# FFN of an encoder trunk: the token operands of the fast matrix product are made between its first products, all first products stand ahead of the other five, and half of the normalising runs on ScalarE and GpSimd

## The chip, the cores and the metric

The kernel runs on one core of a Trainium2 chip. The engines of a core work in parallel, each through its own list of instructions in order: TensorE (PE) multiplies matrices, VectorE (DVE) and ScalarE (ACT) and GpSimd (POOL) work elementwise, and SyncE (SP) issues most DMAs. An instruction that waits holds up all that stands behind it on its engine. The metric is the device time of one execution in microseconds (us), the median of several runs. TensorE's granted clock is shown as a share of full speed; its two levels are 1.2 and 2.4 GHz, so 0.5 and 1.0.

## The reference

Two layers of a hybrid block on x (1 x 1024 tokens x 1024, float32). The part that the change touches is the feed-forward network (FFN):

```python
for i in range(DEPTH):                      # 2 layers
    ...                                     # attention, gating, convolution, w_out
    hf = rms_norm(x, norm_ffn_g[i]) @ w_gate_up[i]          # 1024 x 5632
    x = x + (jax.nn.silu(hf[..., :D_FF]) * hf[..., D_FF:]) @ w_down[i]   # D_FF = 2816
    ...                                     # gate and projection
```

Here `rms_norm(x, g)` is x times the reciprocal root of its mean square per token, times the gain g per column.

## The kernel before

Tiles lie with model columns on the 128 partitions and tokens along the free axis, so x is X[hf][m], m = 0 to 7 (blocks of 128 columns), hf = 0 or 1 (512 tokens each), every X tile 128 x 512. To keep float32 accuracy every operand is split into a high part (a rounded copy) and a low part (the rest), and a product takes three matmuls: high with high (L224), the token's low part with the weight's high part (L226), and the weight's low part with the token's high part (L228).

The product x @ w_gate_up is a seven-product scheme over 2 x 2 blocks: two halves of tokens, two halves of the inner dimension (HK = 4 blocks each), and two neighbouring column blocks. There are NP2 = 11 column pairs, each for the gate and for the up weights.

- **First products.** `first(j)` (L1110) makes two of the seven, for the first half of the tokens and the pair's first column block: two weights (gate, up) x two halves of the inner dimension x 12 matmuls = 48 matmuls, one PSUM bank for each group of 12. These use tokens without the norm's factor (tile hl), so the factor `bc` (one number per token, broadcast over partitions) is multiplied in by DVE while it evicts the bank: L1138 and L1140, then L1141 and L1145 combine. L1143 is the Silu on ACT. The sums go to DRAM (sum_d, act_d). The weights come through `load_w`: a DMA into raw, a high part wh, and a low part wl (L216), by default on ACT (L122) and DVE.
- **The other five.** They need combined token operands, which `token_forms(k)` (L1160) makes for k = 0 to 3: four normalisations of X tiles (L1157, in place: times gain, times bc), subtractions on DVE (L1167, L1169) and POOL (L1168, L1172), and five splits into high and low (tile tf; L122 on ACT and L125 on DVE). `rest(j)` (L1191) combines the raw weights (tile rw, loaded by `load_rest`, L1183) on POOL (L1228 to L1231), splits the results (L122, L125) and makes 5 x 12 matmuls for each of two weights, 120 in all.

The loop around them, per layer, begins in the attention's tail: w_out's second part is applied by `wo_second(0)`, then `first(0)` to `first(3)` (with the flag `ahead`, which has their wl made on POOL and wh on DVE), `first(4)` together with `wo_second(1)`, which ends with the norm of the second half: L292 sums on PE, L268 and L270 make the factor on DVE and POOL, L281 broadcasts it on PE and L298 copies it on ACT. Then come `token_forms(0)` to `token_forms(3)`, `first(5)` to `first(7)` (BEHIND = 3), and then `rest(j)` followed by `first(8 + j)` while there are any. The down product (w_down) follows.

The order of instructions on each engine is fixed when the program is built: a scheduler takes the program's order and the buffers that come free, and moves instructions past each other within that. Pools bound what runs ahead: raw, wh and wl have 3 buffers each, the PSUM pools ps_a and ps_t 3 and 4 banks (tiles pa and pt).

Of the kernel before, what the change touches and what calls it, by code (L numbers as in the profile page):

```python
# [43 lines left out]
PLE_LAG = 2  # L44
NP2 = NF // 2
AHEAD = 4
BEHIND = 3

C1 = 1
C2 = 2.0  # L50
# [21 lines left out]
def tile_encoder_trunk(ctx: ExitStack, tc: tile.TileContext, x, p, positions, norm_mix_g, w_in,  # L72
# [48 lines left out]
    def copy_h(dst, src, scale=1.0):  # L121
        nc.scalar.activation(dst, src, AF.Copy, scale=scale)  # L122
# [71 lines left out]
    def col(nme, layer, k):  # L194
        b, n = col_of[nme]
        c = b + layer * n + k
        return (cols0 if nme == "mix" else cols1)[:, c:c + 1]
# [264 lines left out]
    for layer in range(DEPTH):  # L462
# [656 lines left out]
        def first(j):  # L1119

            hl0, bc = nrm[0].hl, nrm[0].bc
            c0 = 2 * j * P
            ws = [load_w(rows_of(w_gate_up[layer], 0, NK, off + c0, P), (NK, P),
                         nc.gpsimd if ahead else None, nc.vector if ahead else None)
                  for off in (0, DFF)]
            a, sm = T("sg"), U("sm")
            for i, (wh, wl) in enumerate(ws):
                bank = BA if ahead else BU
                s1 = sm[:, HALF[i]]
                for h in range(2):  # L1130
                    b = bank()
                    for k in range(h * HK, (h + 1) * HK):
                        step_mm(b, (wh[:, k, :], wl[:, k, :]), hl0[k], k % HK == 0,
                                k % HK == HK - 1)
                        if k % 2 == 1:
                            bg.tick()
                    if h == 0:
                        nc.vector.tensor_tensor(out=s1, in0=b, in1=bc, op=ALU.mult)  # L1138
                    else:
                        nc.vector.tensor_tensor(out=b, in0=b, in1=bc, op=ALU.mult)  # L1140
                        nc.vector.tensor_tensor(out=b if i else a, in0=b, in1=s1, op=ALU.add)  # L1141
                if i == 0:
                    nc.scalar.activation(a, a, AF.Silu)  # L1143
            nc.scalar.dma_start(out=sum_d[j], in_=sm)
            nc.vector.tensor_tensor(out=a, in0=b, in1=a, op=ALU.mult)  # L1145
            nc.scalar.dma_start(out=act_d[2 * j][:, HALF[0]], in_=a)
# [9 lines left out]
        def normed(hf, m):  # L1156
            nc.vector.scalar_tensor_tensor(out=X[hf][m], in0=X[hf][m], scalar=col("ffn", layer, m),  # L1157
                                           in1=nrm[hf].bc, op0=ALU.mult, op1=ALU.mult)

        def token_forms(k):  # L1160

            for hf in range(2):
                for m in (k, k + HK):
                    normed(hf, m)
            b11, b21, b12, b22 = X[0][k], X[0][k + HK], X[1][k], X[1][k + HK]
            t1 = T("t1")
            nc.vector.tensor_tensor(out=t1, in0=b12, in1=b11, op=ALU.subtract)  # L1167
            nc.gpsimd.tensor_tensor(out=b12, in0=b22, in1=b12, op=ALU.subtract)  # L1168
            nc.vector.tensor_tensor(out=b11, in0=b22, in1=t1, op=ALU.subtract)  # L1169
            forms[0][k] = split(b11)  # L1170
            forms[1][k] = split(b12)
            nc.gpsimd.tensor_tensor(out=b21, in0=b21, in1=b11, op=ALU.subtract)  # L1172
            forms[2][k] = split(t1)
            forms[3][k] = split(b21)
            forms[4][k] = split(b22)
# [85 lines left out]
        first(AHEAD)  # L1261
        wo_second(1)
        ahead = False
        for k in range(HK):
            token_forms(k)
        for j in range(AHEAD + 1, AHEAD + 1 + BEHIND):
            first(j)
        for j in range(NP2):
            load_rest(j)
            rest(j)  # L1270
# [151 lines left out]
```

## Time and profile before

| | |
|---|---|
| median of 3 runs | 2505.62 us (2503.2 to 2507.15) |
| profiled execution, its own time | 2507.3 us |
| its span in the trace | 2505.5 us |
| PE / DVE / ACT / POOL busy | 93% / 60% / 37% / 29% |
| mean granted clock of PE | 0.967 |

The profile is of one execution. Layer 0's FFN runs roughly from 420 to 1090 us, layer 1's from 1655 us. A row of the waits says which engine and line stood idle for which other. In a timeline the number in brackets is the idle time ahead of the row's first instruction, and the arrow what ended it. Instructions that follow each other without a gap overlap at their ends, so the step from start to start, not the duration, counts in a run of them.

### The profile page before, as it was taken

The page shows a single profiled execution, that of the slowest core. Times are in us where ns is not written, and L with a number is a line of the kernel's source. Part 1 is how long each engine was busy: PE and PEld are TensorE (multiplying, and loading weights), DVE is VectorE, ACT ScalarE, POOL GpSimd, SP SyncE. Part 2 cuts the span into 40 slices and gives each one's busy share as a digit, 9 for nine tenths or more (in the row PEclk, how much of TensorE's full clock was granted, in tenths as well). Part 3 has the DMA queues.
Part 4 walks back from the last instruction along what each step waited for, and adds up shares of the span by engine and source line. Part 5 has one row for each costly group of instructions (what it writes and reads, how often), then busy time and mean ns, then how long its engine had stood idle before and what let it go on. Part 6 is the DMA issues. An engine that isn't in the chain of part 4 may idle for free. (4 is left out here: it accounts for less than half of the span.)

```text
span 2505.5 us, 30172 instructions
## 1 busy us (share of the span) xinstructions
PE 2327.1 (93%) x11404; PEld 1950.1 (78%) x11404; DVE 1493.4 (60%) x2307; ACT 915.8 (37%) x1610; POOL 730.1 (29%) x529
## 2 busy tenths in 40 slices
PE   7997977969999999999999898879689999999999
PEld 6996766847788888888789876768577888888887
DVE  7996676475665553626469666755856555526252
ACT  4346572132232243424323455612322222425242
POOL 4122415541344300104321233255424342001031
PEclk9998998989999999999999999989899999999999
DMA  6110513632543245543321123135345341736332
GB/s 200 44 55 9 177 34 97 214 110 93 190 163 110 94 161 174 176 135 106 100 68 39 35 76 110 58 119 181 101 160 173 118 146 52 234 123 210 100 91 70
DMA packets 237010, 294.78 MB, mean 118 GB/s; under 512 B 10644, under 2 KB 180208, under 8 KB 236864
## 3 DMA queue, kind: packets, MB, share of 16 engines
q1 hardware_dynamic: 217696, 248.55, 30.9%
q10 hardware_dynamic: 18688, 44.06, 4.8%
q8 instruction: 90, 1.47, 0.2%
q0 software_dynamic: 480, 0.24, 0.1%
q14 instruction: 56, 0.46, 0.1%
HBM read 228.84 MB, written 63.96 MB: 117 GB/s over the span
## 5 line engine op out<-in xcount | busy, mean ns | idle before, releaser
L216 DVE TENSOR_TENSOR wl<-raw,wh 128x1024 fp32r<-128x1024 f32 x172 | 216.7, 1260 | 255.3 <-ACT wh L122 249.8
L122 ACT ACTIVATE wh<-raw 128x1024 fp32r<-128x1024 f32 x172 | 182.0, 1058 | 438.2 <-PE pt L226 302.5
L226 PE MATMUL pt<-tf,wh 128*128 128x512 f32 x792 | 308.2, 389 | 0.0
L224 PE MATMUL pt<-tf,wh 128*128 128x512 f32 x792 | 306.1, 390 | 0.0
L228 PE MATMUL pt<-tf,wl 128*128 128x512 f32 x792 | 304.6, 389 | 0.0
L224 PE MATMUL pa<-tf,wh 128*128 128x512 f32 x704 | 277.3, 396 | 23.5 <-ACT wh L122 23.5
L264 POOL TENSOR_TENSOR st<-st,sq 128x512 f32<-128x512 f32 x82 | 121.4, 1482 | 596.9 <-ACT sq L263 594.9
L226 PE MATMUL pa<-tf,wh 128*128 128x512 f32 x704 | 278.2, 395 | 0.0
L228 PE MATMUL pa<-tf,wl 128*128 128x512 f32 x704 | 273.4, 393 | 0.0
L224 PE MATMUL pa<-hl,wh 128*128 128x512 f32 x564 | 228.1, 406 | 16.4 <-DVE sg L1141 10.9
L226 PE MATMUL pa<-hl,wh 128*128 128x512 f32 x564 | 225.6, 400 | 2.9 <-DVE hl L128 2.7
L228 PE MATMUL pa<-hl,wl 128*128 128x512 f32 x564 | 223.9, 397 | 0.0
L1228 POOL TENSOR_TENSOR ws<-rw,rw 128x512 f32<-128x512 f32 x44 | 70.1, 1593 | 410.6 <-DMA rw<-in_w_gate_up_dram 214.6
L608 PE MATMUL pa<-wh,hl 128*128 128x256 f32 x640 | 179.9, 287 | 7.0 <-ACT zq L621 3.7
L610 PE MATMUL pa<-wl,hl 128*128 128x256 f32 x640 | 181.9, 286 | 0.2 <-DVE wl L216 0.2
L611 PE MATMUL pa<-wh,hl 128*128 128x256 f32 x640 | 180.9, 286 | 0.0
L224 PEld LDWEIGHTS pa<-tf,wh 128*128 128x128 f32 x704 | 134.7, 191 | 55.1 <-ACT wh L122 26.9
L228 PEld LDWEIGHTS pt<-tf,wl 128*128 128x128 f32 x792 | 148.7, 188 | 31.1
L224 PEld LDWEIGHTS pt<-tf,wh 128*128 128x128 f32 x792 | 148.7, 188 | 30.9
L226 PEld LDWEIGHTS pt<-tf,wh 128*128 128x128 f32 x792 | 148.7, 188 | 30.6
L125 DVE TENSOR_TENSOR wl<-rw,wh 128x512 fp32r<-128x512 f32 x176 | 140.8, 804 | 32.5 <-ACT wh L122 32.4
L228 PEld LDWEIGHTS pa<-tf,wl 128*128 128x128 f32 x704 | 134.2, 191 | 28.6
(320 smaller groups left out, 5029.6 us busy)
## 6 DMA issues: line engine op xcount, KB each, us to landing
rw<-in_w_gate_up_dram SPq DMA_DIRECT2D x88, 512.0 KB, 6.9
raw<-in_w_down_dram SPq DMA_DIRECT2D x88, 512.0 KB, 3.6
raw<-in_w_gate_up_dram SPq DMA_DIRECT2D x44, 512.0 KB, 4.4
ac<-act SPq DMA_DIRECT2D x88, 256.0 KB, 4.3
raw<-in_w_ple_gate_dram SPq DMA_DIRECT2D x32, 512.0 KB, 4.2
raw<-in_w_in_dram SPq DMA_DIRECT2D x28, 512.0 KB, 3.8
raw<-in_w_out_dram SPq DMA_DIRECT2D x24, 512.0 KB, 4.2
sum<-sm ACTq DMA_DIRECT2D x22, 512.0 KB, 5.3
```

The lines of the kernel that those rows point to most:

```text
L122: nc.scalar.activation(dst, src, AF.Copy, scale=scale)
L125: nc.vector.tensor_tensor(out=dst, in0=src, in1=f(h), op=ALU.subtract)
L216: (eng or nc.vector).tensor_tensor(out=l, in0=raw, in1=f(h), op=ALU.subtract)
L224: nc.tensor.matmul(b, lhsT=wh, rhs=hl[:, 0:512], start=first, stop=False, skip_group_check=again)
L226: nc.tensor.matmul(b, lhsT=wh, rhs=hl[:, 512:1024], start=False, stop=False, skip_group_check=again)
L228: nc.tensor.matmul(b, lhsT=wl, rhs=hl[:, 0:512], start=False, stop=last, skip_group_check=again)
L264: (eng or nc.gpsimd).tensor_tensor(out=n.s, in0=n.s, in1=sq, op=ALU.add)
L608: nc.tensor.matmul(o, lhsT=x_[:, th], rhs=wh, start=(kc + k == 0), stop=False)
L610: nc.tensor.matmul(o, lhsT=x_[:, th], rhs=wl, start=False, stop=False)
L611: nc.tensor.matmul(o, lhsT=x_[:, tl], rhs=wh, start=False, stop=(kc == 1 and k == 3))
L1228: tt(out=s3, in0=a21, in1=a22, op=ALU.add)
```

## The change

BEHIND becomes 6, and the loop that comes after `wo_second(1)` makes all eleven first products before the first `rest`. `token_forms(k)` stands after `first(5 + k)` for k = 0 to 3. The first half's eight X tiles are no longer normalised by L1157 on DVE: ACT multiplies by the gain (a copy with a scale per partition, in place) and POOL by the factor (one multiply each, in place). And after the `ahead` part the gate weight's low part is made on POOL; the up weight's stays on DVE.

```diff
-BEHIND = 3
+BEHIND = 6
...
             ws = [load_w(rows_of(w_gate_up[layer], 0, NK, off + c0, P), (NK, P),
-                         nc.gpsimd if ahead else None, nc.vector if ahead else None)
+                         nc.gpsimd if ahead or off == 0 else None, nc.vector if ahead else None)
                   for off in (0, DFF)]
...
         def token_forms(k):
 
-            for hf in range(2):
-                for m in (k, k + HK):
-                    normed(hf, m)
+            for m in (k, k + HK):
+                normed(1, m)
...
         ahead = False
-        for k in range(HK):
-            token_forms(k)
-        for j in range(AHEAD + 1, AHEAD + 1 + BEHIND):
-            first(j)
+        for m in range(NK):
+            copy_h(X[0][m], X[0][m], col("ffn", layer, m))
+            nc.gpsimd.tensor_tensor(out=X[0][m], in0=X[0][m], in1=nrm[0].bc, op=ALU.mult)
+        for n in range(BEHIND):
+            first(AHEAD + 1 + n)
+            if n < HK:
+                token_forms(n)
         for j in range(NP2):
             load_rest(j)
             rest(j)
```

What stands in a row on POOL, in layer 0, where the norm of the first half ends (L270 makes its factor rcol_667; wl_687 and wl_696 are low parts of weights of `first(1)` and `first(2)`). Before:

```order
L264 TENSOR_TENSOR st_323_2500<-st_323_2500,sq_656_3982 128x512
L264 TENSOR_TENSOR st_323_2500<-st_323_2500,sq_662_4009 128x512
L264 TENSOR_TENSOR st_323_2500<-st_323_2500,sq_665_4029 128x512
L270 TENSOR_TENSOR rcol_667_4038<-ms_668_4039,mhalf_158 128x4
L216 TENSOR_TENSOR wl_687_4132<-raw_685_4130,wh_686_4131 128x1024
L216 TENSOR_TENSOR wl_696_4202<-raw_694_4200,wh_695_4201 128x1024
L216 TENSOR_TENSOR wl_699_4208<-raw_697_4206,wh_698_4207 128x1024
L216 TENSOR_TENSOR wl_708_4278<-raw_706_4276,wh_707_4277 128x1024
```

And with the change, where L1265 is the new multiply and st_323 holds the factor:

```order
L264 TENSOR_TENSOR st_323_2500<-st_323_2500,sq_656_3982 128x512
L264 TENSOR_TENSOR st_323_2500<-st_323_2500,sq_662_4009 128x512
L264 TENSOR_TENSOR st_323_2500<-st_323_2500,sq_665_4029 128x512
L270 TENSOR_TENSOR rcol_667_4038<-ms_668_4039,mhalf_158 128x4
L1265 TENSOR_TENSOR X_613_3776<-X_613_3776,st_323_2500 128x512 x2
L1265 TENSOR_TENSOR X_614_3777<-X_614_3777,st_323_2500 128x512 x2
L1265 TENSOR_TENSOR X_615_3778<-X_615_3778,st_323_2500 128x512 x2
L1265 TENSOR_TENSOR X_616_3779<-X_616_3779,st_323_2500 128x512 x2
L216 TENSOR_TENSOR wl_687_4132<-raw_685_4130,wh_686_4131 128x1024
L216 TENSOR_TENSOR wl_696_4202<-raw_694_4200,wh_695_4201 128x1024
L216 TENSOR_TENSOR wl_699_4208<-raw_697_4206,wh_698_4207 128x1024
```

The eight multiplies stand between the norm's factor and the low part wl_687; in the kernel before nothing stood there.

On DVE in layer 0, between the normalisation of the second half and the evictions of the first products that follow it (sm_796 before, and sm_772 with the change, hold the sums of `first(5)`; pa and pt are banks; tf tiles are parts of the token operands). Before, behind eight normalisations, eight subtractions and three low parts of weights:

```order
L1140 TENSOR_TENSOR pt_812_4843<-pt_812_4843,st_323_2500 128x512
L125 TENSOR_TENSOR tf_766_4621<-X_613_3776,tf_766_4621 128x512
L125 TENSOR_TENSOR tf_767_4624<-X_730_4428,tf_767_4624 128x512
L125 TENSOR_TENSOR tf_768_4628<-t1_765_4617,tf_768_4628 128x512
L125 TENSOR_TENSOR tf_769_4631<-X_615_3778,tf_769_4631 128x512
L125 TENSOR_TENSOR tf_770_4634<-X_732_4430,tf_770_4634 128x512
L125 TENSOR_TENSOR tf_772_4645<-X_613_3776,tf_772_4645 128x512
L125 TENSOR_TENSOR tf_773_4648<-X_730_4428,tf_773_4648 128x512
L125 TENSOR_TENSOR tf_774_4652<-t1_771_4641,tf_774_4652 128x512
L125 TENSOR_TENSOR tf_775_4655<-X_615_3778,tf_775_4655 128x512
L1138 TENSOR_TENSOR sm_796_4722<-pt_797_4723,st_323_2500 128x512
L1138 TENSOR_TENSOR sm_796_4722<-pt_799_4753,st_323_2500 128x512
```

With the change, directly behind the same eight normalisations:

```order
L1138 TENSOR_TENSOR sm_772_4642<-pt_773_4643,st_323_2500 128x512
L216 TENSOR_TENSOR wl_788_4735<-raw_786_4733,wh_787_4734 128x1024
L1141 TENSOR_TENSOR sg_771_4641<-pa_774_4657,sm_772_4642 128x512
L1166 TENSOR_TENSOR t1_777_4707<-X_730_4428,X_613_3776 128x512
L1138 TENSOR_TENSOR sm_772_4642<-pt_775_4673,st_323_2500 128x512
L1168 TENSOR_TENSOR X_613_3776<-X_732_4430,t1_777_4707 128x512
L1141 TENSOR_TENSOR pa_776_4687<-pa_776_4687,sm_772_4642 128x512
L216 TENSOR_TENSOR wl_806_4833<-raw_804_4831,wh_805_4832 128x1024
L1145 TENSOR_TENSOR sg_771_4641<-pa_776_4687,sg_771_4641 128x512
L125 TENSOR_TENSOR tf_778_4711<-X_613_3776,tf_778_4711 128x512
L125 TENSOR_TENSOR tf_779_4714<-X_730_4428,tf_779_4714 128x512
L1140 TENSOR_TENSOR pt_794_4785<-pt_794_4785,st_323_2500 128x512
```

An eviction (L1138, L1140, L1141, L1145) now stands after every one to three instructions on the operands; before, nine splits stood in a row ahead of the two L1138.

On SP, at the point where the raw weights of the first `rest` (rw and sm) are loaded; raw tiles are weights of first products or of the down product. Before:

```order
L211 DMA raw_855_5138<-in_w_gate_up_dram 128x8x128
L211 DMA raw_858_5144<-in_w_gate_up_dram 128x8x128
L211 DMA raw_897_5415<-in_w_gate_up_dram 128x8x128
L1184 DMA rw_827_4939<-in_w_gate_up_dram 128x4x256
L1184 DMA rw_828_4940<-in_w_gate_up_dram 128x4x256
L1187 DMA sm_825_4937<-sum0_119 128x1024
L1184 DMA rw_829_4944<-in_w_gate_up_dram 128x4x256
L1184 DMA rw_830_4945<-in_w_gate_up_dram 128x4x256
```

With the change:

```order
L211 DMA raw_837_5021<-in_w_gate_up_dram 128x8x128
L211 DMA raw_840_5027<-in_w_gate_up_dram 128x8x128
L211 DMA raw_849_5097<-in_w_gate_up_dram 128x8x128
L211 DMA raw_852_5103<-in_w_gate_up_dram 128x8x128
L211 DMA raw_1202_7422<-in_w_down_dram 128x1024
L211 DMA raw_1207_7433<-in_w_down_dram 128x1024
L211 DMA raw_1212_7444<-in_w_down_dram 128x1024
L1183 DMA rw_863_5175<-in_w_gate_up_dram 128x4x256
L1183 DMA rw_864_5176<-in_w_gate_up_dram 128x4x256
L1186 DMA sm_861_5173<-sum0_119 128x1024
L1183 DMA rw_865_5180<-in_w_gate_up_dram 128x4x256
L1183 DMA rw_866_5181<-in_w_gate_up_dram 128x4x256
```

The loads of the first `rest` have moved behind all loads of first products and behind three loads of w_down.

## Rows read from the trace of the kernel before

**Rows 1.** The page's first line, its busy times with their shares of the span.
```profile
span 2505.5 us, 30172 instructions
...
PE 2327.1 (93%) x11404; PEld 1950.1 (78%) x11404; DVE 1493.4 (60%) x2307; ACT 915.8 (37%) x1610; POOL 730.1 (29%) x529
```

**Rows 2.** The view of waits for PE over the whole span: engine, tile and line that stood idle, what it waited for, us in total, times, longest.
```profile
PE pt L224 <- DVE sm L1138: 36.9, 2, 18.6
PE pa L224 <- ACT wh L122: 23.5, 8, 4.2
...
PE pa L224 <- DVE sg L1141: 10.9, 3, 5.3
```

**Rows 3.** The table by stretches: start and end, length, then busy time (and number of instructions) of PE, PE's weight loads, DVE, ACT and POOL, the granted clock, DMA share and GB/s.
```profile
506.30:902.50 396.20, 366.67 (x1591) 300.47 (x1590) 244.21 (x342) 112.32 (x186) 143.18 (x96) 0.97 0.36 123
1741.50:2139.10 397.60, 366.37 (x1593) 300.97 (x1593) 248.88 (x343) 112.37 (x186) 142.95 (x96) 0.97 0.36 123
700.00:870.00 170.00, 170.00 (x752) 140.76 (x751) 92.50 (x144) 47.09 (x81) 71.35 (x52) 1.00 0.33 114
...
640.00:650.00 10.00, 8.82 (x32) 7.14 (x33) 9.16 (x9) 2.31 (x4) 8.61 (x6) 0.83 0.17 68
```

**Rows 4.** PE's timeline, the rows of layer 0's up-projection that begin after idle time: start, duration, engine, line, operation and tiles, and in brackets the idle time and its releaser.
```profile
535.88 0.76 PE L224 MATMUL pt<-hl,wh 128*128 128x512 f32 x1 [18.29 <-DVE sm L1138]
...
556.06 0.80 PE L224 MATMUL pa<-tf,wh 128*128 128x512 f32 x1 [3.94 <-ACT wh L122]
...
598.95 0.50 PE L224 MATMUL pa<-tf,wh 128*128 128x512 f32 x1 [2.97 <-ACT wh L122]
...
641.17 0.74 PE L224 MATMUL pa<-tf,wh 128*128 128x512 f32 x1 [2.21 <-ACT wh L122]
...
682.95 0.50 PE L224 MATMUL pa<-tf,wh 128*128 128x512 f32 x1 [1.80 <-ACT wh L122]
```

**Rows 5.** DVE's timeline in layer 0 from the broadcast of the second half's norm to the eviction that PE waits for.
```profile
507.22 5.39 DVE L1157 SCALAR_TENSOR_TENSOR X<-X,cols,st 128x512 f32<-128x512 f32 x8 [0.87 <-ACT st L298]
...
521.35 2.82 DVE L125 TENSOR_TENSOR tf<-X,tf 128x512 fp32r<-128x512 f32 x2
524.10 1.75 DVE L125 TENSOR_TENSOR tf<-t,tf 128x512 fp32r<-128x512 f32 x1
...
533.85 0.68 DVE L125 TENSOR_TENSOR tf<-t,tf 128x512 fp32r<-128x512 f32 x1
534.45 0.68 DVE L125 TENSOR_TENSOR tf<-X,tf 128x512 fp32r<-128x512 f32 x1
535.05 1.27 DVE L1138 TENSOR_TENSOR sm<-pt,st 128x512 f32<-128x512 f32 x2
```

**Rows 6.** POOL's timeline in layer 0: three elementwise operations, two low parts of weights, and the first subtractions of the token operands.
```profile
405.18 3.96 POOL L264 TENSOR_TENSOR st<-st,sq 128x512 f32<-128x512 f32 x3
...
422.76 2.78 POOL L216 TENSOR_TENSOR wl<-raw,wh 128x1024 fp32r<-128x1024 f32 x1 [8.15 <-DVE wh L215]
...
437.17 2.40 POOL L216 TENSOR_TENSOR wl<-raw,wh 128x1024 fp32r<-128x1024 f32 x1 [4.73 <-DVE wh L215]
...
513.29 13.67 POOL L1168 TENSOR_TENSOR X<-X,X 128x512 f32<-128x512 f32 x4 [7.44 <-DVE t L1167]
```

**Rows 7.** The table by stretches around the first half's normalisation, columns as in rows 3.
```profile
425.90:431.20 5.30, 0.01 (x1) 0.01 (x1) 5.30 (x10) 0.03 (x1) 1.12 (x1) 0.85 0.34 100
431.20:440.00 8.80, 8.80 (x28) 7.01 (x29) 4.39 (x7) 1.24 (x2) 3.65 (x2) 0.70 0.31 91
```

**Rows 8.** DVE's timeline around the first half's normalisation in layer 0, and the row of layer 1 that answers to the second.
```profile
420.62 1.41 DVE L1157 SCALAR_TENSOR_TENSOR X<-X,cols,st 128x512 f32<-128x512 f32 x2
...
422.54 3.55 DVE L1157 SCALAR_TENSOR_TENSOR X<-X,cols,st 128x512 f32<-128x512 f32 x2
...
426.62 2.72 DVE L1157 SCALAR_TENSOR_TENSOR X<-X,cols,st 128x512 f32<-128x512 f32 x4
...
437.68 0.69 DVE L1141 TENSOR_TENSOR sg<-pa,sm 128x512 f32<-128x512 f32 x1
...
1657.87 3.55 DVE L1157 SCALAR_TENSOR_TENSOR X<-X,cols,st 128x512 f32<-128x512 f32 x2
```

**Rows 9.** PE's timeline around the statistics of the second half's norm in layer 0.
```profile
503.61 0.94 PE L292 MATMUL po<-ones,st 128*128 128x1 f32 x8
...
505.91 0.65 PE L281 MATMUL pt<-ident,rcol 128*128 128x128 f32 x4 [0.30 <-POOL rcol L270]
```

**Rows 10.** POOL's timeline: the first combination of weights of the second `rest` in layer 0.
```profile
594.25 1.29 POOL L1228 TENSOR_TENSOR ws<-rw,rw 128x512 f32<-128x512 f32 x1 [38.61 <-DMA rw<-in_w_gate_up_dram]
```

**Rows 11.** The page's DMA issues: tiles, queue, number, KB each, median us from issue to landing.
```profile
rw<-in_w_gate_up_dram SPq DMA_DIRECT2D x88, 512.0 KB, 6.9
raw<-in_w_down_dram SPq DMA_DIRECT2D x88, 512.0 KB, 3.6
```

**Rows 12.** ACT's timeline: the copy of the first half's broadcast factor in layer 0.
```profile
418.79 0.59 ACT L298 COPY st<-pt 128x512 f32<-128x512 f32 x1 [6.04 <-PE pt L281]
```

**Rows 13.** The costliest groups of the page, POOL's combinations of weights: number, busy us, mean ns of one, idle before.
```profile
L1228 POOL TENSOR_TENSOR ws<-rw,rw 128x512 f32<-128x512 f32 x44 | 70.1, 1593 | 410.6 <-DMA rw<-in_w_gate_up_dram 214.6
```

## The prediction

> **What bounds the kernel now.** I read the page's shares first: TensorE (PE) is busy 93% of the span, VectorE (DVE) 60%, GpSimd (POOL) 29% [rows 1]. So time is won only where PE stands still or runs at its half clock, and I looked next for those places. The view of waits, taken for PE over the whole span, names three that belong to the FFN [rows 2]: a bank that DVE frees late by L1138 (36.9 us in two waits), weights that ScalarE (ACT) brings late by L122 (23.5 us in eight), and banks that wait for DVE's L1141 (10.9 us in three). The program runs the layer twice, so each is one place per layer or four.
>
> PE's stream shows the places in layer 0 [rows 4]: 18.29 us before 535.88, and then 3.94, 2.97, 2.21 and 1.80 us, each at the start of the five other products of a column pair (tile tf). The table by stretches gives what they cost [rows 3]. From 700 to 870 us PE has no idle time: 752 products in 170.00 us, 0.226 us each. The FFN's up-projection from 506.3 us (the end of the second half's norm broadcast) to 902.5 us (the first down product) holds 1591 of them: 1591 x 0.226 = 359.6 of 396.2 us, so 36.6 us are lost in layer 0; in layer 1 1593 x 0.226 = 360.0 of 397.6, so 37.6. The waits that are listed make only some 30 of each; the rest is the half clock behind them. Where 2.21 us of idle stand, the stretch of 640 to 650 us has 32 products in 8.82 us of busy time at a granted clock of 0.83: 32 x 0.226 = 7.2, so 1.6 us more are gone. I take 1.7 us for each gap of 2 to 4 us, and nothing for shorter ones.
>
> Why the 18 us: DVE's stream [rows 5] has eight normalisations (5.39 us), then subtractions and splits for all four sets of token operands, and the two evictions (L1138 at 535.05) for which PE waits stand behind them. They are also slow there: POOL's four subtractions of 513.29 take 13.67 us [rows 6] where three like operations at 405.18 took 3.96, and DVE's splits beside them 2.82 for two and 1.75 for one, where 533.85 to 535.05 shows a step of 0.60.
>
> A second place lies before it, in wo_second: the 5.30 us before 431.2 us, then 28 products in 8.80 us at clock 0.70 [rows 7]; 28 x 0.226 = 6.3, so 2.5 more, 7.8 us in all. There DVE normalises the first half (eight L1157, two of them 3.55 us instead of 1.41), with evictions queued behind [rows 8]. Layer 1 has the same 3.55 row.
>
> **The change, part by part.** *Normalising the first half leaves DVE.* Eight L1157 per layer, 1.41 + 3.55 + 2.72 us [rows 8], go. With them the 5.30 us of idle go, since the evictions are no longer behind them. ACT's eight scaled copies cost nothing: the order puts three of them ahead of the second half's norm work, and five fit in ACT's 6.04 us of idle before the broadcast's copy at 418.79 [rows 12]. POOL's eight multiplies begin when that copy is done, 419.4, and the order shows them ahead of the low part of the next weight (wl_687). At 1.30 each (3.96 / 3) they end at 429.8, the low part (2.40 uncontended) at 432.2 [rows 6]. PE, without its idle, has from 425.9 a whole bank (12 products) and six products that need only the high part: 18 x 0.226 = 4.1, so it waits from 430.0 to 432.2. With a little lengthening of POOL beside DVE's casts and of the clock I put 3.5 us against 7.8: a gain of 4.3 per layer. Bounds: no wait left (gain 7.8), and POOL held at the 3.42 us of 513.29 for all eight, 449.2 + 2.4 less 430.0 = 19 to 22 us (a loss of some 13).
>
> *Token operands between first products.* From the broadcast to the last first product PE now has 21 banks, 252 products, 57.0 us. I went down DVE's new order with the steps of before: 8 normalisations at 0.67, 28 subtractions and splits at 0.60, five low parts at 1.2, 32 evictions at 0.61: 5.4 + 16.8 + 6.0 + 19.5 = 47.7. Without contention DVE reaches each eviction 3 to 8 us before PE needs its bank. The tightest with POOL's work in front of it is the fourth column's first bank: DVE at 33.2, PE at 37.6, 4.4 of slack, and about 15 us of POOL's own work (four low parts, now POOL's for the gate, at 2.4, and four or five subtractions at 1.27) before it; at the last bank 48.2 against 56.6, slack 8.4, and 19.8 of POOL's work.
>
> What DVE loses beside POOL no row tells exactly. In 513.29 to 526.93 POOL had 5.2 us of own work and DVE lost 2.7 (2.82 + 1.75 for three steps of 0.60), half of it. Beside the low part at 422.76 (2.78 against 2.40) it lost 2.1, 3.55 against 1.41: nearly all of it [rows 6, 8]. Evictions from PSUM beside POOL's work were not slower: 0.69 at 437.68 [rows 8], inside POOL's 2.40 from 437.17 [rows 6]. I take one half, the row with the same operations: 7.6 less 4.4 = 3.2 us of PE's time. Ends: 0, and all of it.
>
> The Trainium skill, "SBUF — State Buffer", section "Who interferes with whom", says that a DVE instruction with two SBUF inputs and a GpSimd one that reads SBUF take turns at a shared port pair, the second blocked for the whole of the first. The 3.55 row agrees; at 513.29, where POOL lost 8.5 us itself, the cost is shared. By the rule alone DVE would lose up to all of POOL's time, the first rival below.
>
> *The norm's statistics.* Four products that stood between L292 and L281 while DVE and POOL worked out the factor [rows 9] stand elsewhere now: 4 x 0.226 = 0.9 us of idle.
>
> *Entry to the other five.* Before, each column pair's remaining products followed a first(8+j); the first four pairs began with a wait. Now all eleven stand together, as at 700 to 870 us, so I cost ten of the entries at nothing: the raw weights come while the pair before it runs. The first entry remains. The order puts three w_down loads ahead of the rw loads on SP's queue, and the third waits for the buffer of the last up weight, whose low part DVE makes at 44.6 without and about 53.5 with contention. An rw load lands 6.9 us later (median) [rows 11], 60.4; from POOL's first combination to PE's first product 4.7 us pass (594.25 to 598.95) [rows 4, 10]: 65.1. PE is through at 57.0 + 0.9 + 3.2 = 61.1. So 4.0 us of stall, and 1.7 of half clock. If the three w_down loads of 3.6 us delay rw one after the other, up to 8 us more; with a quick landing next to nothing.
>
> **Sum.** Left over per layer: 0.9 + 3.2 + 4.0 + 1.7 = 9.8 us. Layer 0: 36.6 - 9.8 + 4.3 = 31.1; layer 1: 37.6 - 9.8 + 4.3 = 32.1; together 63.2. The profiled execution took 2507.3 us over its span of 2505.5; its span becomes 2442.3 and its time 2444.1. Its time is 1.7 above the median of the runs, 2505.62, so I forecast 2505.6 - 63.2 = 2442.
>
> **Rivals.**
> (a) DVE is blocked for all of POOL's time. The loss before the last bank is 19.8 - 8.4 = 11.4 instead of 3.2, in two gaps of over 2 us (3.4 us of half clock), and the early wait grows by some 2.4: 14.0 per layer, 2442 + 28 = 2470. For it: the 3.55 row; against: the shared cost at 513.29. 20%.
> (b) The rw loads come late behind w_down: 8 us per layer, 2458. For it: SP's order; against: they are only delayed if DVE or the queue is. 17%.
> (c) Everything is hidden: per layer only 0.9 and 1 to 2 us of entry and early wait remain, about 2422. For it: DVE's slack at each bank. 8%.
> (d) Slower: GpSimd becomes the bound. Its multiplies stand ahead of a weight that PE waits for, and its gate low parts feed the first products. At 2.63 times their lone price (3.42 / 1.30) with DVE blocked throughout, the early place loses about 13 and the later one still gains about 13: no change, 2505. Above that factor the kernel is slower: at 3.5, POOL's 19.8 us become 69 for PE's 57, another 12 per layer, and the early place loses some 9 more than at 2.63: 21 per layer less is 2547. For it: 13.67 us for four; against: at the early place DVE then has mostly evictions and casts, and POOL's combinations of weights, of the same shape and beside DVE's splits, take 1.59 in the mean of 44 [rows 13]. 4%.
> (e) The change does not do what it says: the order has the operands between the first products and no first product behind a remaining one, so it does; what can still be is a scheduler's shift in layer 1's attention, a few us either way. 1%.
>
> **How the numbers follow.** The forecast has 50%. Eight times in ten: from 2424, a little above (c), to 2476, past (a); (d) and the tails are left out. What a measurement of this kernel can tell is about 0.2%, 5 us; (a), (b), (c) and the forecast all lie far below that line: faster 0.95, same 0.02, slower 0.03.
>
> **What will show it.** Right: the wait on L1138 of 18 us is gone in both layers, the ones on L122 shrink from eight to two; POOL's eight multiplies take 10 to 13 us; the stretch from broadcast to down product is 370 us or less, of it the remaining products about 11 x 27.1 = 298 without a gap; one wait at their start. Wrong: multiplies of 2 us and more with PE waiting for the low part behind them, waits of PE for evictions adding up to over 8 us per layer among the first products, an entry wait over 8 us, or new gaps between the pairs.

## The result and the profile after

The changed kernel takes 2445.27 us in the median of four runs (2441.96 to 2445.79), the kernel before 2506.39 beside it (2503.2 to 2508.02): a ratio of 0.9755 with a 95% interval of 0.9738 to 0.9772, so 61 us less. The forecast was 2442 us. The profiled execution took 2445.79 us with a span of 2444.0.

The page's first lines and the view of waits for PE over the whole span, which answer to [rows 1, 2]:

```profile
span 2444.0 us, 30173 instructions
...
PE 2314.7 (95%) x11404; PEld 1942.1 (79%) x11404; DVE 1452.7 (59%) x2279; ACT 925.5 (38%) x1626; POOL 757.3 (31%) x557
```

```profile
PE pa L224 <- ACT wh L122: 11.1, 2, 6.2
...
PE pa L224 <- DVE sg L1141: 4.7, 3, 1.6
...
PE pa L228 <- POOL wl L216: 2.7, 2, 1.4
...
PE pt L228 <- DVE wl L216: 2.4, 1, 2.4
...
PE pa L224 <- DVE sm L1138: 1.9, 4, 1.1
```

The 36.9 us behind L1138 have become 1.9 us, in four short waits instead of two of 18 us. The 23.5 us behind L122 have become 11.1, one wait per layer, at the entry to the other five products. The waits on POOL's and DVE's low parts (L216) are new. In layer 0 the rows of PE that answer to [rows 4, 7, 9]:

```profile
431.54 0.50 PE L224 MATMUL pa<-hl,wh 128*128 128x512 f32 x1 [1.57 <-DVE sg L1141]
433.64 0.80 PE L228 MATMUL pa<-hl,wl 128*128 128x512 f32 x1 [1.37 <-POOL wl L216]
...
504.15 0.65 PE L281 MATMUL pt<-ident,rcol 128*128 128x128 f32 x4 [1.35 <-POOL rcol L270]
527.58 0.50 PE L224 MATMUL pa<-hl,wh 128*128 128x512 f32 x1 [0.31 <-DVE sm L1138]
...
540.78 0.50 PE L224 MATMUL pa<-hl,wh 128*128 128x512 f32 x1 [1.09 <-DVE sm L1138]
...
556.05 0.50 PE L224 MATMUL pa<-hl,wh 128*128 128x512 f32 x1 [0.90 <-DVE sg L1145]
...
573.47 0.79 PE L224 MATMUL pa<-tf,wh 128*128 128x512 f32 x1 [6.22 <-ACT wh L122]
```

The table by stretches, columns as in [rows 3]: the two up-projections, then in layer 0 all first products behind the broadcast, their first ten microseconds, the early place, and the other five products with the ten microseconds at their start.

```profile
504.80:876.18 371.38, 362.86 (x1589) 298.20 (x1588) 233.96 (x337) 112.22 (x186) 142.91 (x100) 0.99 0.38 131
1706.23:2077.50 371.27, 362.35 (x1589) 298.46 (x1588) 234.35 (x338) 112.40 (x186) 141.29 (x100) 0.99 0.39 131
...
504.80:567.24 62.44, 60.14 (x252) 47.73 (x251) 61.36 (x77) 24.33 (x36) 21.29 (x12) 0.97 0.45 146
504.80:515.00 10.20, 10.20 (x39) 8.28 (x39) 9.55 (x12) 3.91 (x5) 2.14 (x1) 0.83 0.11 34
420.61:440.00 19.39, 16.45 (x64) 12.86 (x65) 9.75 (x14) 2.55 (x3) 17.66 (x11) 0.91 0.31 99
573.47:875.00 301.53, 301.53 (x1331) 249.62 (x1332) 170.05 (x258) 85.91 (x147) 117.19 (x85) 0.99 0.35 122
573.47:583.47 10.00, 10.00 (x37) 8.15 (x38) 8.14 (x10) 1.62 (x3) 7.70 (x6) 0.84 0.91 308
```

The up-projection has gone from 396.2 and 397.6 us to 371.4 and 371.3. From 573.47 on PE has no idle time: the entries to the later pairs cost nothing. In the first products DVE is busy 61.36 of 62.44 us, so it has next to nothing to spare there, though PE waits for it only 2.3 us.

How the gain is spread over the program is best seen from fixed points of PE's stream, each taken from the start of a row of PE's timeline: *a* the attention's last broadcast before the FFN (L281 from the tile ar), *b* the broadcast of the second half's norm (L281 at 505.91 in [rows 9]), *c* the first down product, *d* the first statistics broadcast behind the down products; the last column goes to the start of PE's last row. Lengths in us for layer 0 and, from a of layer 1 on, layer 1:

| kernel | start to a | a to b (early place) | b to c (up-projection) | c to d | d to a of layer 1 | a to b | b to c | c to PE's last row |
|---|---|---|---|---|---|---|---|---|
| before | 405.2 | 100.7 | 396.6 | 250.1 | 487.6 | 101.0 | 397.7 | 361.4 |
| changed | 405.9 | 98.3 | 372.0 | 250.2 | 480.8 | 98.5 | 371.9 | 361.5 |
| order_only | 403.4 | 100.7 | 365.8 | 250.1 | 483.5 | 99.3 | 366.1 | 361.4 |
| norm_only | 406.3 | 97.5 | 399.2 | 250.1 | 482.1 | 97.5 | 400.1 | 361.4 |
| gate_dve | 402.9 | 97.4 | 366.1 | 250.2 | 484.2 | 97.6 | 366.2 | 361.4 |
| rw_early | 403.5 | 98.1 | 369.9 | 250.1 | 481.4 | 98.6 | 370.0 | 361.4 |
| pool_dummy | 402.5 | 97.0 | 379.3 | 250.2 | 481.0 | 97.7 | 376.5 | 361.5 |
| gate_rw | 405.0 | 97.4 | 369.4 | 250.1 | 481.4 | 97.2 | 366.0 | 361.5 |
| gate_wl1 | 407.7 | 91.7 | 365.8 | 250.1 | 481.6 | 92.6 | 367.0 | 361.4 |
| all_three | 404.4 | 92.4 | 370.2 | 250.1 | 488.6 | 92.5 | 366.3 | 361.4 |
| before_again | 403.2 | 100.4 | 393.9 | 250.2 | 484.4 | 100.4 | 398.8 | 361.4 |
| after_again | 403.6 | 98.1 | 373.7 | 250.1 | 482.5 | 98.4 | 372.0 | 361.4 |

The rows below the second are the experiments that follow; the last two are the two kernels once more, unchanged, and show how far a length varies by itself: up to 2.7 us in the up-projection (396.6 and 393.9 for the kernel before). Of the 61.5 us by which the spans differ, the up-projection gives 24.6 and 25.8, the early place 2.4 and 2.5, and 6.8 come from the stretch between d and layer 1's attention, in which nothing was changed; the start took 0.7 us longer.

### The profile page after: what moved, and what is told of

Same layout as the page of the kernel before. It is cut to its first block, busy times and chain, and to the rows that moved or that the text cites. A ratio compares the mean times of both kernels' runs of the same rounds, so it can differ in the third digit from the quotient of the medians.

```text
span 2444.0 us, 30173 instructions
## 1 busy us (share of the span) xinstructions
PE 2314.7 (95%) x11404; PEld 1942.1 (79%) x11404; DVE 1452.7 (59%) x2279; ACT 925.5 (38%) x1626; POOL 757.3 (31%) x557
## 5 line engine op out<-in xcount | busy, mean ns | idle before, releaser
L216 DVE TENSOR_TENSOR wl<-raw,wh 128x1024 fp32r<-128x1024 f32 x160 | 203.0, 1269 | 260.8 <-ACT wh L122 254.2
L122 ACT ACTIVATE wh<-raw 128x1024 fp32r<-128x1024 f32 x172 | 181.8, 1057 | 392.8 <-PE pt L226 260.9
L224 PE MATMUL pa<-tf,wh 128*128 128x512 f32 x704 | 274.0, 392 | 11.1 <-ACT wh L122 11.1
L226 PE MATMUL pa<-tf,wh 128*128 128x512 f32 x704 | 275.4, 391 | 0.0
L226 PEld LDWEIGHTS pt<-tf,wh 128*128 128x128 f32 x792 | 148.7, 188 | 30.8
L216 POOL TENSOR_TENSOR wl<-raw,wh 128x1024 fp32r<-128x1024 f32 x56 | 138.2, 2473 | 69.3 <-ACT wh L122 46.0
L122 ACT ACTIVATE wh<-rw 128x512 fp32r<-128x512 f32 x176 | 105.6, 622 | 141.3 <-PE pt L226 73.9
```

What stands on the lines that cost most here:

```text
L216: (eng or nc.vector).tensor_tensor(out=l, in0=raw, in1=f(h), op=ALU.subtract)
L224: nc.tensor.matmul(b, lhsT=wh, rhs=hl[:, 0:512], start=first, stop=False, skip_group_check=again)
L226: nc.tensor.matmul(b, lhsT=wh, rhs=hl[:, 512:1024], start=False, stop=False, skip_group_check=again)
```

## The experiments

**The order alone** (order_only), against the changed kernel:

```diff
-                         nc.gpsimd if ahead or off == 0 else None, ...
+                         nc.gpsimd if ahead else None, ...
...
-            for m in (k, k + HK):
-                normed(1, m)
+            for hf in range(2):
+                for m in (k, k + HK):
+                    normed(hf, m)
...
-        for m in range(NK):
-            copy_h(X[0][m], X[0][m], col("ffn", layer, m))
-            nc.gpsimd.tensor_tensor(out=X[0][m], in0=X[0][m], in1=nrm[0].bc, op=ALU.mult)
```

> Only the new order: all first products ahead with the token operands between them; both halves are normalised by L1157 on DVE and the gate's low parts stay on DVE. Theory: the order alone removes the 18 us in front of the late eviction and the three entries to the other five; the early place stays as before (5.3 us of idle and some 2.5 us of half clock per layer instead of the 1.6 + 1.4 us of idle and 2 to 3 us of half clock of the changed kernel), so 3 to 4 us per layer are given up: 2451 to 2453 us. Rival 1: without the relief of DVE by eight normalisations and four low parts the evictions are late again, with waits of PE of more than 5 us per layer among the first products: 2460 us or more. Rival 2: the normalising is worth nothing: 2445 us.

2438.5 us (2436.85 to 2440.87), ratio to before 0.9729 (0.9714 to 0.9743): less than the changed kernel (2441.96 to 2445.79), against all three expectations. The early place kept its 5.30 us of idle, as expected, and its 100.7 us (99.3 in layer 1). But the up-projection takes 365.8 us, 6.2 less than in the changed kernel. So the order alone gains 30.8 us there in layer 0, where the changed kernel gains 24.6: something else in the change gives some 6 us per layer back.

**The normalising alone** (norm_only): the ACT copies and POOL multiplies in the kernel before, with its old order.

```diff
+        for m in range(NK):
+            copy_h(X[0][m], X[0][m], col("ffn", layer, m))
+            nc.gpsimd.tensor_tensor(out=X[0][m], in0=X[0][m], in1=nrm[0].bc, op=ALU.mult)
         for k in range(HK):
             token_forms(k)
...
-            for hf in range(2):
-                for m in (k, k + HK):
-                    normed(hf, m)
+            for m in (k, k + HK):
+                normed(1, m)
```

> Only the moved normalising, in the old order: ACT's scaled copies and POOL's eight multiplies in place of the first half's L1157. Theory: the wait of 5.3 us in the early place shrinks to some 3 us in two parts, the waits of 18 us and the four entry waits per layer stay: 3 to 4 us per layer less than before, 2499 us (2496 to 2503). Rival: POOL's multiplies only move the wait from the eviction to the low part of the weight: 2506 us, no change.

2498.39 us (2495.29 to 2502.63), ratio 0.9971 (0.9958 to 0.9984), the time that the theory gave. The early place is shorter by 3.2 and 3.5 us as expected. The up-projection is longer by 2.6 and 2.4 us, which was not expected; as it varies by up to 2.7 us between the two traces of the kernel before, whether the edit has a part in it stays open. In this trace 5.5 us come from the stretch d to a, on which more below, so that the time came out as the theory gave it may in part be luck.

**The gate's low parts back on DVE** (gate_dve): the changed kernel without one of its edits.

```diff
-                         nc.gpsimd if ahead or off == 0 else None, nc.vector if ahead else None)
+                         nc.gpsimd if ahead else None, nc.vector if ahead else None)
```

> The changed kernel with the gate's low parts of the later first products on DVE again. Theory of exclusive turns (a POOL operation on SBUF holds up a DVE operation with two SBUF inputs until it ends): each low part on POOL costs DVE about 2 us of its 2.4 when it falls on such an operation, and 1.2 us when DVE makes it itself, so moving them gains nothing: 2445 us, within 4 us, and in the trace the eight subtractions on POOL delay DVE but no row of DVE's of 2.7 us or more is left. Rival: POOL's work runs mostly beside DVE's evictions from PSUM and is nearly free, so giving DVE six more low parts of 1.2 us per layer makes its evictions late: 4 to 6 us per layer more waiting of PE, 2453 to 2457 us.

2435.93 us (2432.53 to 2438.42), ratio 0.9717 (0.9702 to 0.9731), and its interval lies below that of the changed kernel. Neither expectation had this sign of that size: the edit that takes work from DVE costs 5.9 us of the up-projection in layer 0 and 5.7 in layer 1. The first products behind the broadcast in layer 0, the table by stretches of this run, of order_only and (above) of the changed kernel:

```profile
500.97:559.75 58.78, 57.71 (x252) 46.80 (x251) 57.93 (x81) 23.62 (x35) 13.55 (x10) 1.00 0.53 173
```

```profile
504.78:562.46 57.68, 57.67 (x252) 46.81 (x251) 56.85 (x81) 23.62 (x35) 14.56 (x10) 1.00 0.53 175
```

252 products take 58.78 and 57.68 us instead of 62.44; DVE makes four more low parts (81 instructions for 77) and is busy 3.4 and 4.5 us less. Most of the reason stands in the changed kernel's own rows. DVE's timeline:

```profile
513.10 2.71 DVE L1166 TENSOR_TENSOR t<-X,X 128x512 f32<-128x512 f32 x1
515.74 0.68 DVE L1138 TENSOR_TENSOR sm<-pt,st 128x512 f32<-128x512 f32 x1
516.34 1.39 DVE L1168 TENSOR_TENSOR X<-X,t 128x512 f32<-128x512 f32 x1
...
523.71 3.21 DVE L125 TENSOR_TENSOR tf<-X,tf 128x512 fp32r<-128x512 f32 x2
...
546.25 1.22 DVE L216 TENSOR_TENSOR wl<-raw,wh 128x1024 fp32r<-128x1024 f32 x1
```

and POOL's beside it:

```profile
512.86 2.40 POOL L216 TENSOR_TENSOR wl<-raw,wh 128x1024 fp32r<-128x1024 f32 x1 [8.76 <-ACT wh L122]
515.89 1.28 POOL L1167 TENSOR_TENSOR X<-X,X 128x512 f32<-128x512 f32 x1 [0.63 <-DVE t L1166]
...
523.37 2.40 POOL L216 TENSOR_TENSOR wl<-raw,wh 128x1024 fp32r<-128x1024 f32 x1 [4.27 <-ACT wh L122]
...
546.71 3.02 POOL L216 TENSOR_TENSOR wl<-raw,wh 128x1024 fp32r<-128x1024 f32 x1 [3.40 <-ACT wh L122]
```

POOL's low part ends at 512.86 + 2.40 = 515.26, and the subtraction that DVE began at 513.10 ends at 515.81, 0.55 later: it stood still for all of POOL's instruction and then ran its usual 0.6. The next one, L1168, ends at 517.73, 0.56 after POOL's end of 517.17; the first of the two splits at 523.71 waits for POOL's 525.77. The eviction from PSUM at 515.74, of which POOL's 515.89 covers all but the start, took its usual 0.68. POOL keeps its lone price of 2.40 and 1.28 where it began first; where DVE did, as with the low part of 546.25, POOL is the one that waits (3.02 us from 546.71). Adding up by how much DVE's rows in this stretch exceed their usual lengths (0.68 us for one operation of 128x512, 0.60 more for each that follows in the row, 1.22 for a low part; the eight L1157 take 5.39 us here, in gate_dve and in the kernel before, POOL standing idle beside them, and are left out) gives 11.4 us for POOL's 21.3, and in gate_dve, where no operation of 2.7 us is left among the first products, 3.8 us for 13.6.

Not all of the 5.9 us is this. The edit also changed PE's order at the broadcast. In gate_dve, as in order_only and in the kernel before [rows 9], four products stand between the statistics' matmuls (L292) and L281; in the changed kernel none do. L281 waits 1.35 us there, and in gate_dve:

```profile
500.32 0.65 PE L281 MATMUL pt<-ident,rcol 128*128 128x128 f32 x4 [0.30 <-POOL rcol L270]
```

The wait itself belongs to a to b. The half clock behind it, 39 products at 0.83 in the table above, costs 1.4 us of the 5.9. Of the rest, 2.2 us are the entry to the other five (4.00 us of idle instead of 6.22) and 1.2 the waits among the first products (1.07 instead of 2.30); some 1 us was not traced further.

Against order_only, which differs only in the place of the first half's normalising, gate_dve is 2.6 us faster. The runs of the two overlap, but a to b is 3.3 and 1.7 us shorter.

**POOL work that nobody waits for** (pool_dummy): gate_dve, with two operations added on POOL after each of the six first products. They write to a tile whose values are not used again, so the output stays the same.

```diff
+            if not ahead:
+                s = nrm[1].s
+                for i in range(2):
+                    nc.gpsimd.tensor_tensor(out=s, in0=s, in1=sm[:, HALF[i]], op=ALU.subtract)
             nc.scalar.dma_start(out=sum_d[j], in_=sm)
```

> The gate's low parts on DVE, as in the run gate_dve (2436 us), and two more operations of 128x512 on POOL after each of the six later first products, which subtract that product's sums from a tile that nobody reads any more; no other engine waits for them. They are 12 x 1.27 = 15.2 us of POOL's time per layer, about what the six low parts were (6 x 2.4). Theory: POOL's operations cost by holding up DVE's operations with two inputs in SBUF; what DVE loses between the broadcast and the first of the other five rises from 5 to about 10 to 13 us per layer, and the time from the broadcast to the first down product from 366 to 369 to 372 us: 2442 to 2447 us. Rival: the low parts cost because PE and SP wait for them, made later and slower on POOL; operations that nobody waits for cost nothing: 2436 us, 366 us.

2453.77 us (2452.07 to 2455.73), ratio 0.9798 (0.9783 to 0.9813). That is 18 us over gate_dve for operations whose results no engine reads, so the rival, by which such operations cost nothing, falls. L281 waits 0.30 us here as in gate_dve, so PE's order at the broadcast has no part in it. It is more than expected: the up-projection takes 379.3 and 376.5 us instead of 366. The row that shows it, the first products in layer 0:

```profile
500.17:568.20 68.03, 61.47 (x252) 49.21 (x251) 65.51 (x81) 24.46 (x36) 29.13 (x19) 0.93 0.50 165
```

The same 81 instructions of DVE take 65.51 us instead of 57.93, 7.6 more for 15.6 more of POOL's: DVE is held up. PE's granted clock falls to 0.93 there, with idle time that has come between the products, and behind it the entry waits 6.76 us. One thing stays mixed in this run: POOL's subtractions for the token operands stand behind the added operations in its queue, so a part of the 18 us may be their lateness and not DVE's.

**The loads of the first rest earlier** (rw_early), in the changed kernel:

```diff
         for n in range(BEHIND):
+            if n == BEHIND - 3:
+                load_rest(0)
             first(AHEAD + 1 + n)
...
         for j in range(NP2):
-            load_rest(j)
+            if j:
+                load_rest(j)
             rest(j)
```

> The changed kernel with the loads of the first of the other five (rw and sm) called three first products earlier, so that SP issues them ahead of the three w_down loads. Theory: the entry wait (6.2 us in layer 0, 4.9 us in layer 1) and the half clock behind it (some 1.6 us each) go: 14 us less than the changed kernel, 2431 us. Rival: the entry waits for POOL's combinations and the splits, which DVE's and POOL's other work hold up, and not for the load: 2445 us, the wait on L122 stays.

2442.78 us (2439.77 to 2445.67), ratio 0.9749 (0.9733 to 0.9765): not told apart from the changed kernel. The 6.22 us in front of the other five are gone in layer 0 (in layer 1 3.03 of the 4.92 stay), and these have come in their place (PE's timeline):

```profile
547.72 0.50 PE L224 MATMUL pa<-hl,wh 128*128 128x512 f32 x1 [2.41 <-DVE sm L1138]
...
563.76 0.79 PE L224 MATMUL pa<-hl,wh 128*128 128x512 f32 x1 [2.83 <-DVE sg L1141]
```

The second has to do with the first rest, whose combinations on POOL now run among the first products, from 553.32 on: beside them DVE's two splits at 558.52 take 2.38 us instead of 1.28 and a low part at 561.42 takes 1.69 instead of 1.22, ahead of the eviction. The first comes before that. Its eviction stands behind a split that POOL's low part of a gate weight held up:

```profile
544.22 2.85 DVE L125 TENSOR_TENSOR tf<-X,tf 128x512 fp32r<-128x512 f32 x1
```

```profile
544.14 2.38 POOL L216 TENSOR_TENSOR wl<-raw,wh 128x1024 fp32r<-128x1024 f32 x1 [3.40 <-ACT wh L122]
```

In the changed kernel splits were held up at that place too (3.50 us for two at 547.38), and PE did not wait; why it does here stays open. The way from the broadcast to the first of the other five takes 68.9 us here and 69.3 in the changed kernel. The wait was for the load, as the theory said; but DVE, which is full, comes late all the same, and nearly all of the stall has only moved.

**Both together, the gate's low parts on DVE and the loads earlier** (gate_rw), gave 2434.22 us (2432.2 to 2435.25), ratio 0.9719 (0.9704 to 0.9733).

> The run gate_dve with the loads of the first of the other five issued ahead of the w_down loads. In rw_early the entry wait went and the same time came back as waits for evictions, DVE being full. Theory: with the low parts on DVE, DVE still is busy nearly all of that stretch (57.9 of 58.8 us), so most of the 4.0 us of entry wait and 1.6 us of half clock per layer comes back as late evictions: 2432 to 2436 us. Rival: DVE has now enough slack, the entry wait goes for good: 2425 us (5.6 us per layer).

The theory held, by two mechanisms. In layer 0 the time comes back as late evictions (a wait of 4.4 us on L1141, and 1.82 stay at the entry). In layer 1 the entry still waits 3.50 us, and there POOL was done with the combination long before. The rows of POOL, ACT and PE:

```profile
1756.94 1.63 POOL L1230 TENSOR_TENSOR rw<-rw,rw 128x512 f32<-128x512 f32 x1
```

```profile
1762.14 0.63 ACT L1143 ACTIVATE sg<-sg 128x512 f32<-128x512 f32 x1 [3.46 <-DVE sg L1141]
1762.68 1.13 ACT L122 ACTIVATE wh<-rw 128x512 fp32r<-128x512 f32 x2
```

```profile
1763.87 0.80 PE L224 MATMUL pa<-tf,wh 128*128 128x512 f32 x1 [3.50 <-ACT wh L122]
```

The high part of the first combined weight stands on ACT behind the Silu of the last first product, which waits for DVE's eviction of PE's last banks. So with this order on ACT, earlier weights alone do not take these 3.5 us away.

**One low part off POOL's queue** (gate_wl1): gate_dve, and wl_687, the low part behind POOL's eight multiplies, on DVE.

```diff
-                         nc.gpsimd if ahead else None, nc.vector if ahead else None)
+                         nc.gpsimd if ahead and not (j == 1 and off) else None, nc.vector if ahead else None)
```

> The run gate_dve with the low part of the second first product's up weight (wl_687, the one behind POOL's eight multiplies) on DVE. Theory: PE's wait for that low part (1.38 us) and part of the half clock behind it go; 2 to 3 us per layer: 2430 to 2433 us. Rival: on DVE the low part is held up by POOL's multiplies and holds up the evictions behind it, so the wait of 1.57 us on the eviction grows by as much: 2436 us or a little more.

2423.23 us (2420.3 to 2425.04), ratio 0.9673 (0.9654 to 0.9691): the best of all, 22 us under the changed kernel, and with 5.7 and 5.0 us per layer in its place twice the gain expected. Here the early place is whole, in the table by stretches:

```profile
422.00:440.00 18.00, 18.00 (x81) 14.90 (x80) 13.79 (x19) 2.55 (x3) 18.00 (x11) 1.00 0.43 143
```

No idle time and clock 1.00, where the changed kernel has 64 products in 19.39 us at 0.91. The low part takes DVE 1.72 us (at 423.33, usual 1.2), and the eviction behind it is not late enough to matter. Both of PE's waits are gone. With the low part in time the scheduler no longer pulls six products that need only high parts ahead of it, of which two had waited for a bank (the 1.57 us on L1141). With the waits the half clock behind them went, and a to b fell by 5.7 and 5.0 us.

**All three edits** (all_three):

> gate_dve with both edits, the earlier loads of the first of the other five and the low part of wl_687 on DVE. If both edits work by themselves their gains add, down to 2420 us; by the theories that DVE is the limit in both places 2430 to 2436 us.

2429.15 us (2428.12 to 2432.66), ratio 0.9702 (0.9686 to 0.9718), above gate_wl1 and near what the theories of a full DVE gave: the earlier loads cost 4.4 us in layer 0's up-projection (370.2 against 365.8; in gate_rw against gate_dve 3.3), and its trace has the longest stretch d to a, 488.6 us.

**Both kernels once more, unchanged,** for the 6.8 us of that stretch.

> The kernel before once more, unchanged, for a second trace. Open is 6.9 us of the gain: between layer 0's end of the down product and layer 1's attention (from the first statistics broadcast behind the down product at 1152.69 us to the one behind layer 1's attention at 1640.32 us) the kernel before took 487.6 us and the changed one 480.8, though nothing there is changed. Theory: that stretch varies from one execution to the next, so a second execution lies elsewhere between 481 and 489 us. Rival: it belongs to the program's order, and repeats within 1 us.

> The changed kernel once more, unchanged, for a second trace. Theory: the stretch of 480.8 us varies between executions, 481 to 489 us, with the rest of the trace the same to 1 us. Rival: it repeats within 1 us, and the order made the difference.

In a second trace of the kernel before (2499.34 us) the stretch took 484.4 us, 3.2 less than in the first; in one of the changed kernel (2446.66 us) 482.5, 1.7 more. So it varies by itself, by more than the rival allows. The traces of the eight other kernels lie at 481.0 to 488.6. Two traces each leave a difference of 4.4 us in the mean, 486.0 against 481.6; whether the order of the program has a part in it stays open. Nor does the rest repeat to 1 us, as was expected of the changed kernel: its up-projection in layer 0 took 1.7 us more in the second trace, and its start 2.3 less. By the two second traces the spans differ by 52.7 us instead of 61.5.

## Why the prediction was right

The sum was 63.2 us and the spans differ by 61.5, but the terms do not all bear this out. The parts that the prediction costed gave 24.6 + 25.8 + 2.4 + 2.5 = 55.3 us; the other 6 came from a stretch that it set at nothing, and at least some of them are chance. That the number came so close is partly luck. Of the signs it named, one was missed by a little: the stretch from broadcast to down product is 371.4 and 371.3 us, not 370 or less.

*The 18-us wait.* Right in place, cause and size: it is gone in both layers, and the order alone removes it.

*The entries to the other five.* Right that ten of them cost nothing: PE is busy all of 573.47 to 875.00. The first was undersized: 6.22 and 4.92 us of idle instead of 4.0, and 1.6 of half clock (37 products, 8.4 us of work, in the first 10.00) as predicted. The steps were right: the third w_down load waits on SP's queue for the last low part and holds rw back behind it.

```profile
547.49 13.00 SPq L211 DMA_DIRECT2D raw<-in_w_down_dram  x3
560.54 0.97 SPq L1183 DMA_DIRECT2D rw<-in_w_gate_up_dram  x2
```

rw is issued 55.7 us behind the broadcast's end (predicted 53.5), POOL begins at 568.81, 8.3 us later (predicted 6.9), and from there to PE's 573.47 it is 4.66 (predicted 4.7).

*DVE beside POOL.* The size was near: 11.4 of POOL's 21.3 us lost, where the prediction took one half; PE's waits came to 2.3 us in layer 0 and 4.0 in layer 1 for the 3.2 predicted. The picture behind the half was wrong. DVE and POOL do not share: a DVE operation with two inputs in SBUF stands still for the whole of POOL's instruction, as the first rival had it and as the Trainium skill, "SBUF — State Buffer", section "Who interferes with whom", says (this trace agrees: 0.55 us from POOL's end to DVE's, again and again). The rival's price of 2470 was too high for another reason: nearly half of POOL's time fell on evictions from PSUM, which ran on. That section leaves it to the order of issue who waits, and the row of 546.71, where POOL came second, agrees with it too (3.02 us instead of 2.40). It does not settle who comes next when both have work in a row: at 513.29 in the kernel before it was mostly POOL that stood still, 13.67 us for four operations [rows 6].

*Behind the broadcast.* The four products that stood between L292 and L281 were costed at 0.9 us of idle, measured 1.35 against 0.30, 1.05 more. But the half clock behind that gap was left out: 39 products, 8.8 us of work, take the first 10.20 us of the stretch at clock 0.83, 1.4 us per layer. They have to do with the gate's low parts on POOL: without that edit the four products stay where they were. The prediction's price of nothing for a gap shorter than 2 us failed here, and so it did in the early place; its price of 1.7 us for one of 2 to 4 us failed too, as a gap of 2.40 us in layer 1 cost no clock (rows in the last section).

*The early place.* The gain was put at 4.3 us per layer, less the 0.9 behind it 3.4, and is 2.4 and 2.5. POOL's eight multiplies took 11.37 us, in place of 10.4, and the low part came as forecast:

```profile
419.91 11.37 POOL L1265 TENSOR_TENSOR X<-X,st 128x512 f32<-128x512 f32 x8 [4.67 <-ACT st L298]
431.23 7.04 POOL L216 TENSOR_TENSOR wl<-raw,wh 128x1024 fp32r<-128x1024 f32 x3
```

PE's idle there is 1.57 + 1.37 us, and 64 products, 14.5 us of work, fill 19.39: 4.9 us are left instead of the 3.5 assumed. A wait on L1141 stayed that the prediction had struck out. Of the six products that need only high parts the last two go into a bank that DVE frees with the L1141 it begins at 430.79; the prediction counted this bank as free.

*What the prediction never asked* is whether each edit pays by itself. It took the costs of contention off a large gain, and did not ask whether the gate's low parts on POOL were worth theirs: without that edit the rest of the change is 9 us faster. The case that GpSimd becomes the bound did not come; its operations mostly held their lone prices (among the first products at most 1.66 us for 1.3 and 3.02 for 2.4).

## What to carry to other kernels

Where independent products wait for an operand that another engine makes in a long row, spread the row between the products: here the order alone did more than the whole change. Work moved from VectorE to GpSimd is not taken from VectorE when both read two operands from SBUF: count GpSimd's duration as VectorE's loss wherever VectorE then has such work (here 11.4 of 21.3 us), and move it only beside work on PSUM. Look also at what an edit does to the order elsewhere: here it took four products out of a wait. And an engine with little idle time in front of a stall (DVE at 98% of the stretch here) turns every earlier load into a later eviction: take work off it first.

## What the runs showed of the hardware that was not expected

Short gaps can cost TensorE's clock, and the length of a gap does not tell whether it will. Two waits of 1.57 and 1.37 us, 0.7 us apart, left 24 products with 7.09 us of busy time at a granted clock of 0.80, in place of 24 x 0.226 = 5.4 us. The 1.35 us between the statistics' small matmuls and the broadcast cost 1.4 us more behind them, while the single gap of 1.80 us between long runs of products [rows 4] cost nothing that shows, and neither did one of 2.40 us in layer 1 of the changed kernel: the ten microseconds behind it hold 44 products at clock 1.00. The stretch behind the two waits, and then the single gap with the stretch behind it:

```profile
431.54:440.00 8.46, 7.09 (x24) 5.43 (x25) 0.92 (x2) 0.63 (x1) 6.73 (x3) 0.80 0.46 132
```

```profile
1741.24 0.50 PE L228 MATMUL pt<-hl,wl 128*128 128x512 f32 x1 [2.40 <-DVE wl L216]
```

```profile
1741.24:1751.24 10.00, 10.00 (x44) 8.26 (x45) 10.00 (x13) 5.25 (x8) 4.75 (x3) 1.00 0.51 140
```

And two executions of one program can differ by 3 us in a stretch of 480, by itself enough to hide or to feign an effect of an edit elsewhere; lengths between fixed points of PE's stream tell more than the whole time. Two of them repeat within 0.3 us (250.1 and 361.4 above in all kernels); where PE waits often they vary as well, as the 396.6 and 393.9 us of the kernel before show.
